# Mask searches that alternate between ScalarE and VectorE, batched transposes and value products, and moved buffers in a two-layer trunk on one core

## The chip, the core and the metric

The kernel runs on one core of a Trainium2 chip. The metric is the device time of one execution in microseconds (us). Engines are named as in the profile: PE is TensorE's matmuls, PEld its weight loads, DVE is VectorE, ACT is ScalarE, POOL is GpSimd, SP is the engine that issues the DMAs.

## What is computed

The input is 2048 tokens of 1024 floats. Layer 0 runs a state-space scan and a convolution module side by side. Layer 1, where the change lies, is sparse attention: a small indexer scores every key for every query, each query keeps its best 256 admissible keys, and attention with 16 query heads over 4 key heads runs on the kept keys alone. Both layers add to their input, and a final norm follows. In short, for layer 1:

```python
isc = relu(einsum("bqhd,bsd->bqhs", qib, ki))        # 8 index heads
score = einsum("bqh,bqhs->bqs", wib, isc)            # -inf beyond the query's chunk of 64
_, idx = top_k(score, 256)
logits = einsum("bqhgd,bqkhd->bqhgk", qb, k[idx]) * 64 ** -0.5
p = softmax(where(valid, logits, -inf))
ob = einsum("bqhgk,bqkhd->bqhgd", p, v[idx])
h = h + (ob * silu(z)) @ w_out
```

## The kernel before

**Stages.** Layer 0 fills about the first third of the span. Layer 1 then works on two halves of 1024 tokens and on 16 query tiles (tile i holds 128 queries and sees (i+1)*128 keys). It projects index queries and keys for half 0 and half 1 (`project_half` with `first`), and, in the same stretch, scores tiles 2 to 15 (`index_scores`) and searches the masks of tiles 2 to 11 (`select_mask`); the other projections (k, v, q, z; `rest`) are emitted after that and fill PE in between. Then comes attention (`Attend`), with the masks of tiles 12 to 15 (`late`) searched beside it, and the output projection (`layer1_out`).

**Who orders the work.** The Tile framework's scheduler puts the instructions of each engine in an order, by readiness and by their place in the program; on the chip each engine then runs its list in that order. `k.after` adds an order between two instructions without a semaphore. Generators mix streams: `index` steps up to three running masks and every second turn the scoring; in attention `weights` steps `late` once for every `PACE` = 800 columns reduced (two columns are counted for each one reduced), 140 steps (`EARLY`) lie ahead of the first unit.

**Mask search** (`select_mask`, L940 to L1055). The score's 32 bits become two 16-bit keys, `khi` and `klo`. The 256th largest key is found bit by bit: count the keys at or above a threshold, and lower the threshold if there are fewer than needed; 16 bits and one more count for each key, so 34 counts a mask. Tiles not in `ON_ACT` count on DVE (L977) and do two small steps per bit on POOL (L69). Tiles 3, 5, 7, 9, 11 and 13 count on ACT with Sign (L994) and do both small steps on ACT too (L1002, L1004). A tail of DVE operations makes the mask (scan at L1048) and stores it.

**Attention** (`Attend`). A unit is one query tile, one pair of key heads (kp) and one pair of query heads (hp): 64 units, each for two key heads e and two query heads h. `weights` multiplies scores into PSUM (L1117), reduces and adds the mask on DVE (L1121), and takes exp on ACT (L1132). `values`, one unit later, goes over groups of two key blocks: four transposes into a PSUM bank (L1148), a copy to SBUF by ACT (L1153; for the largest tiles every second one by DVE, L1151), four products with v (L1155) that use half the array's columns each, in pairs. All products of a unit sum into one bank of the pool `pv`, which has one buffer; `ps_ot`, the transposed output (L1163), takes the same buffer. The transposes' pool `pt` has three banks. SBUF pools are opened and closed like a stack on the left and the right side, so a buffer that lies where an earlier one was waits for that one's last reader. The key and value buffers of half 0 (`kva0`, `kva1`) lie left, where the index stage's buffers were, and are loaded behind the `EARLY` steps; those of half 1 (`kvb0`, `kvb1`) lie first on the right.

Of the kernel before, what the change touches and what calls it, by code (L numbers as in the profile page):

```python
# [23 lines left out]
P = 128  # L24
L = 2048
# [752 lines left out]
def project_half(k, h, hT, new, order, A, h1_d, S, st, rope, ident, identr, vec, pools):  # L778
# [165 lines left out]
def select_mask(k, i, sc, ip, width, chains, mask_d, pace=None, scalar=False):  # L944

# [14 lines left out]
    cnt, rej, th, k2, cl, least, back = (sv[:, a:a + 1] for a in range(7))  # L960
# [32 lines left out]
    def signs(src, nu):  # L993
        nc.scalar.activation(eq, src, AF.Sign, bias=nu, accum_out=cnt)  # L994

    def search_scalar(src, nu):

        nc.vector.memset(nu, 0.5 - 32768.0)
        for b in range(15, -1, -1):
            signs(src, nu)  # L1000
            yield
            nc.scalar.activation(rej, cnt, AF.Sign, bias=least)  # L1002
            yield
            nc.scalar.activation(nu, rej, AF.Identity, bias=nu, scale=-(2.0 ** (b - 1)))  # L1004
            yield
        nc.scalar.activation(rej, nu, AF.Identity, bias=back)
        yield
        signs(src, rej)
        yield

    if scalar:
        nc.vector.memset(back, -0.5)
        nc.vector.memset(least, nk - 2.0 * KSEL + 0.5)
        yield from search_scalar(hi, th)
        k.vts(th, th, -1.0, ALU.mult)
        k.vts(k2, cnt, -0.5, ALU.mult, KSEL - 0.5 * nk, ALU.add)
        k.vts(least, cnt, 2.0 * nk - 2.0 * KSEL + 0.5, ALU.add)
# [5 lines left out]
    if scalar:  # L1023
# [461 lines left out]
```

## Time and profile before

| | us |
|---|---|
| median of 3 runs | 3014.05 (3012.71 to 3017.12) |
| the profiled execution | 3015.91 |
| its span in the profile | 3014.1 |

| engine | busy us in the span | share |
|---|---|---|
| PE | 2753.4 | 91% |
| PEld | 2220.8 | 74% |
| DVE | 2072.8 | 69% |
| ACT | 1733.2 | 58% |
| POOL | 1105.6 | 37% |

The profiled execution is 1.9 us above the median, and 1.8 us of it lie outside the span. Busy time is the union of an engine's instructions; matmul ends are modelled, so the distance between starts is what tells what a matmul costs. An engine's share over the whole span says little here, since stages have different limits; the rows below are by stretch.

### The profile page before, as it was taken

The page shows a single profiled execution, that of the slowest core. Times are in us where ns is not written, and L with a number is a line of the kernel's source. Part 1 is how long each engine was busy: PE and PEld are TensorE (multiplying, and loading weights), DVE is VectorE, ACT ScalarE, POOL GpSimd, SP SyncE. Part 2 cuts the span into 40 slices and gives each one's busy share as a digit, 9 for nine tenths or more (in the row PEclk, how much of TensorE's full clock was granted, in tenths as well). Part 3 has the DMA queues.
Part 4 walks back from the last instruction along what each step waited for, and adds up shares of the span by engine and source line. Part 5 has one row for each costly group of instructions (what it writes and reads, how often), then busy time and mean ns, then how long its engine had stood idle before and what let it go on. Part 6 is the DMA issues. An engine that isn't in the chain of part 4 may idle for free. (4 is left out here: it accounts for less than half of the span.)

```text
span 3014.1 us, 47682 instructions
## 1 busy us (share of the span) xinstructions
PE 2753.4 (91%) x17488; PEld 2220.8 (74%) x17488; DVE 2072.8 (69%) x3735; ACT 1733.2 (58%) x3558; POOL 1105.6 (37%) x1517
## 2 busy tenths in 40 slices
PE   7789998799999999899889968999989999999998
PEld 5667786678999899899779946666655555666787
DVE  8899986995354556644897479734489997456444
ACT  4122332344243688888768957899965666655311
POOL 3946133732232697745774113321232121001000
PEclk9899999899999999999999979999999999999999
DMA  3254563346566323235322261111110101001332
GB/s 134 76 126 142 157 171 63 122 160 208 172 203 226 97 82 120 64 94 175 99 71 82 88 229 38 58 33 37 38 52 26 47 21 53 22 4 50 123 126 98
DMA packets 233385, 300.40 MB, mean 100 GB/s; under 512 B 14144, under 2 KB 171072, under 8 KB 233024
## 3 DMA queue, kind: packets, MB, share of 16 engines
q1 hardware_dynamic: 233152, 297.37, 31.4%
q8 instruction: 137, 2.24, 0.3%
q14 instruction: 96, 0.79, 0.1%
HBM read 194.16 MB, written 105.25 MB: 99 GB/s over the span
## 5 line engine op out<-in xcount | busy, mean ns | idle before, releaser
L114 POOL TENSOR_TENSOR wl<-wst,wh 128x512 fp32r<-128x512 f32 (+1 forms) x220 | 341.5, 1556 | 444.6 <-ACT wh L113 407.9
L121 PE MATMUL ps_tm<-wh,hb 128*128 128x256 f32 (+1 forms) x1536 | 439.3, 290 | 11.7 <-ACT ot L875 6.9
L122 PE MATMUL ps_tm<-wh,hb 128*128 128x256 f32 (+1 forms) x1536 | 444.4, 290 | 0.8 <-DVE hb L72 0.8
L123 PE MATMUL ps_tm<-wl,hb 128*128 128x256 f32 (+1 forms) x1536 | 439.9, 289 | 0.0
L1132 ACT ACTIVATE lm<-lm,mx 128x512 f32<-128x512 f32 (+15 forms) x256 | 309.1, 1209 | 135.0 <-DVE mx L1121 134.4
L1153 ACT COPY pT<-ps_pt 128x512 f32<-128x512 f32 (+1 forms) x512 | 273.6, 563 | 153.0 <-PE ps_pt L1148 127.0
L72 DVE SCALAR_TENSOR_TENSOR cvo<-hc,vec,cvo 128x1024 f32<-128x1024 f32 x240 | 356.0, 1514 | 0.8
L1121 DVE CUSTOM_DVE_ANT_0 lm<-ps_s,amb 128x1024 f32<-128x1024 f32 (+7 forms) x256 | 249.6, 985 | 152.2 <-PE ps_pt L1148 89.4
L1155 PE MATMUL ps_pv<-pT,v 128*64 128x256 f32 x2176 | 339.1, 399 | 14.6 <-DVE avt L62 8.6
L1148 PEld LDWEIGHTS ps_pt<-ident,lm 128*128 128x128 f32 x2176 | 240.1, 141 | 143.1 <-issue 125.0
L1148 PE MATMUL ps_pt<-ident,lm 128*128 128x128 f32 x2176 | 340.8, 282 | 1.8 <-ACT lm L1132 0.7
L1117 PE MATMUL ps_s<-kh,qs 128*128 128x512 f32 (+2 forms) x640 | 268.6, 421 | 48.7 <-DVE mx L1121 42.1
L121 PEld LDWEIGHTS ps_tm<-wh,hb 128*128 128x128 f32 x1536 | 296.2, 194 | 19.6 <-ACT ot L875 9.0
L69 POOL TENSOR_SCALAR sv<-sv 128x1 f32<-128x1 f32 x512 | 185.6, 363 | 321.6 <-DVE eq L977 282.9
L122 PEld LDWEIGHTS ps_tm<-wh,hb 128*128 128x128 f32 x1536 | 298.0, 194 | 6.0 <-DVE hb L72 1.5
L123 PEld LDWEIGHTS ps_tm<-wl,hb 128*128 128x128 f32 x1536 | 296.7, 194 | 4.3
L113 ACT CAST wh<-wst 128x512 fp32r<-128x512 f32 (+1 forms) x220 | 133.2, 609 | 283.2 <-DMA wst<-in_w_in 131.3
L121 PE MATMUL ps_p<-hh,wh 128*128 128x512 f32 x640 | 256.8, 404 | 18.9 <-ACT uT L520 16.5
L123 PE MATMUL ps_p<-hl,wh 128*128 128x512 f32 x640 | 256.9, 404 | 0.0
L122 PE MATMUL ps_p<-hh,wl 128*128 128x512 f32 x640 | 255.9, 400 | 0.0
L977 DVE TENSOR_SCALAR_CACHE_REDUCE eq<-klo,sv 128x384 bf16<-128x384 uint16 (+7 forms) x136 | 207.0, 1525 | 63.5 <-POOL sv L69 62.8
L977 DVE TENSOR_SCALAR_CACHE_REDUCE eq<-khi,sv 128x384 bf16<-128x384 uint16 (+7 forms) x136 | 206.8, 1525 | 48.7 <-POOL sv L69 47.4
(333 smaller groups left out, 6335.2 us busy)
## 6 DMA issues: line engine op xcount, KB each, us to landing
wst<-in_w_in SPq DMA_DIRECT2D x168, 256.0 KB, 2.9
zs_d<-zt SPq DMA_DIRECT2D x16, 512.0 KB, 3.3
zt<-zs_d SPq DMA_DIRECT2D x16, 512.0 KB, 4.4
ry<-rec_d SPq DMA_DIRECT2D x16, 512.0 KB, 4.2
xr<-in_x SPq DMA_DIRECT2D x16, 512.0 KB, 4.4
wst<-in_w_out SPq DMA_DIRECT2D x32, 256.0 KB, 3.4
h_d<-xr SPq DMA_DIRECT2D x16, 512.0 KB, 3.7
xt<-h_d SPq DMA_DIRECT2D x16, 512.0 KB, 5.7
```

The source lines that it names most:

```text
L72: self.nc.vector.scalar_tensor_tensor(out=out, in0=a, scalar=s, in1=b, op0=op0, op1=op1)
L114: nc.gpsimd.tensor_tensor(out=lo, in0=st, in1=hi.bitcast(F32), op=ALU.subtract)
L121: t.matmul(ps, a[0], b[0], start=start, stop=False)
L122: t.matmul(ps, a[1], b[0], start=False, stop=False)
L123: t.matmul(ps, a[0], b[1], start=False, stop=stop)
L977: op = nc.vector.tensor_scalar(out=eq, in0=src, scalar1=u, scalar2=0.0, op0=op, op1=ALU.add, accum_out=cnt)
L1117: nc.tensor.matmul(pss[e][:, cols], qs[e][:, 2 * hp + h], src[:, e, cols], start=part == 0, stop=part == 1)
L1121: self.pace[0] = nc.vector.tensor_tensor_reduce(out=prob[e][h][:, c:c + w], in0=pss[e][:, 0:w], in1=mb[:, c:c + w], scale=-0.125, scalar=( ...
L1132: nc.scalar.activation(lm, lm, AF.Exp, bias=mxs[e, h][:, nh - 1:nh], scale=-1.0, accum_out=t["den"][:, hd:hd + 1])
L1148: nc.tensor.transpose(ps[:, s, h], prob[e][h][:, (b + s) * P:(b + s + 1) * P], ident)
L1153: nc.scalar.copy(pT[:, 0:n], ps[:, 0:n].rearrange("p s h q -> p s (h q)"))
L1155: nc.tensor.matmul(po[64 * s:64 * s + 64, e], self.kvt[(b + s) // 8, kp][2][:, (b + s) % 8, e * 64:e * 64 + 64], pT[:, s], start=b == 0, s ...
```

## The change

Four edits, all in layer 1.

1. **Search.** There is no `ON_ACT` any more. In every mask the odd bits count on ACT with Sign, and their two small steps are on DVE; the even bits and the last count are on DVE, with their small steps on POOL as before. ACT's small steps are gone.
2. **Batches.** `values` takes the groups two at a time (`TURN` = 2). The transposes of a batch come first, then the products of the batch before it; `k.after` holds the first product behind the batch's last transpose, and the next batch's first transpose, also that of the next unit, behind the last product.
3. **Output transposes.** `ps_ot` takes a bank of `pt` in place of the one bank of `pv`.
4. **Buffers and order.** The norm's input tiles become pairs in a pool of two that stays open; the keys of half 0 for kp = 0 take over these two pairs, and are loaded ahead of the `EARLY` steps. v for kp = 0 lies on the right side, loads after the first unit's queries, then the keys and v of kp = 1. The first two tiles run kp = 0 both before kp = 1. On the right side the small pools of attention come first and the half-1 keys last.

```diff
@@ project_half
-            tiles = []
-            for i in range(2):
-                xt = xp.tile([P, D], F32, tag="xt", name="xt1")
+            pair = xp.tile([P, 2, D], F32, tag="xt", name="xt1")
+            tiles = [pair[:, i] for i in range(2)]
+            for i, xt in enumerate(tiles):
                 r0 = h * HALF + (grp * 2 + i) * P
                 nc.sync.dma_start(xt, h1_d[r0:r0 + P])
-                tiles.append(xt)
@@ select_mask
-    def search(src, u, need):
-        nc.vector.memset(u, 32768.0)
+    def search(src, u, need, most):
+        nc.vector.memset(u, 32767.5)
         for b in range(15, -1, -1):
-            count(src, u, ALU.is_ge)
-            yield
-            k.vts(rej, cnt, need, ALU.is_lt, -float(1 << b), ALU.mult, eng=nc.gpsimd)
-            yield
-            k.vts(u, rej, float(1 << (b - 1)) if b else 0.0, ALU.add, u, ALU.add, eng=nc.gpsimd)
+            step = (-float(1 << b), float(1 << (b - 1)) if b else 0.5)
+            if b % 2:
+                nc.scalar.activation(eq, src, AF.Sign, scale=-1.0, bias=u, accum_out=cnt)
+                yield
+                k.vts(rej, cnt, most, ALU.is_gt, step[0], ALU.mult)
+                yield
+                k.stt(u, rej, step[1], u, ALU.add, ALU.add)
+            else:
+                count(src, u, ALU.is_ge)
+                yield
+                k.vts(rej, cnt, need, ALU.is_lt, step[0], ALU.mult, eng=nc.gpsimd)
+                yield
+                k.vts(u, rej, step[1], ALU.add, u, ALU.add, eng=nc.gpsimd)
             yield
...
-    if scalar:
...
-        yield from search_scalar(hi, th)
...
-    else:
-        yield from search(hi, th, KSEL)
-        k.vts(k2, cnt, -1.0, ALU.mult, KSEL, ALU.add)
+    yield from search(hi, th, KSEL, nk - 2.0 * KSEL)
+    k.vts(k2, cnt, -1.0, ALU.mult, KSEL, ALU.add)
+    k.vts(most, cnt, 2.0, ALU.mult, nk - 2.0 * KSEL, ALU.add)
@@ Attend.values
+        def turned(group):
+            e, b = group
...
+                    op = nc.tensor.transpose(ps[:, s, h], prob[e][h][:, (b + s) * P:(b + s + 1) * P], ident)
+                    if self.held is not None:
+                        k.after(op, self.held)
+                        self.held = None
...
+        def weighted(groups, last):
+            for e, b, n, pT, _ in groups:
...
+                    if last is not None:
+                        k.after(op, last)
+                        last = None
+            self.held = op
+        groups = [(e, b) for e in range(2) for b in range(0, nb, 2)]
+        before = None
+        for g in range(0, len(groups), TURN):
+            now = [turned(group) for group in groups[g:g + TURN]]
+            if before:
+                weighted(before, now[-1][4])
+            before = now
+        weighted(before, None)
...
-        ps = self.pv_.tile([P, 2, 2, 128], F32, tag="pv", name="ps_ot")
+        ps = self.pt.tile([P, 2, 2, 128], F32, tag="pt", name="ps_ot")
@@ layer1
-ON_ACT = (3, 5, 7, 9, 11, 13)
+TURN = 2
...
+        xp = pool(ctx, "xp1", 2, side="right")
...
-            xp = pool(c2, "xp1", 4, side="right")
...
-            for kp in range(2):
-                open_kv(0, kp, pool(ctx, f"kva{kp}", 1))
+            kva = pool(ctx, "kva1", 1)
+            open_kv(0, 1, kva, kva)
...
             half(0, False, rest)
+            open_kv(0, 0, xp)
+            load_k(0, 0)
             for _ in range(EARLY):
                 next(beside)
-            load_kv(0)
         with ExitStack() as c3:
-            open_kv(1, 0, pool(c3, "kvb0", 1, side="right"))
-            open_kv(1, 1, pool(c3, "kvb1", 1, side="right"))
-            pp0 = pool(c3, "pp0", 4, side="right")
...
+            qsp, tm = pool(c3, "qsp", 1, side="right"), pool(c3, "tm", 1, side="right")
...
+            v00 = pool(c3, "kva0", 1, side="right").tile([P, 8, 128], F32, name="v00")
...
-            halves = [(i, kp) for i in ORDER for kp in range(2)]
+            a, b = ORDER[0:2]
+            halves = [(a, 0), (b, 0), (a, 1), (b, 1)] + [(i, kp) for i in ORDER[2:] for kp in range(2)]
...
             load(0)
+            load_v(0, 0)
             ready(0)
+            load_k(0, 1)
+            load_v(0, 1)
```

## Rows read from the trace of the kernel before

**Rows 1.** The page of the profile, its line of busy time, share of the span and instructions of each engine, and its line on the chain of waits that ended last, shares by engine.
```profile
PE 2753.4 (91%) x17488; PEld 2220.8 (74%) x17488; DVE 2072.8 (69%) x3735; ACT 1733.2 (58%) x3558; POOL 1105.6 (37%) x1517
...
PE 20%; DVE 6%; issue 3%; POOL 1%; DMA 0%; ACT 0%; DVEq 0%; ACTq 0%; POOLq 0%
```

**Rows 2.** Busy time by stretch (from:to in us, length, then busy us and instructions of PE, PEld, DVE, ACT, POOL, granted clock of TensorE as a share, DMA share, GB/s). From the top: index stage and first projections, two stretches of the remaining projections, the passage into attention, attention while masks are still searched beside it, attention after that, output projection.
```profile
1000.00:1410.00 410.00, 382.36 (x2889) 365.03 (x2889) 232.11 (x504) 346.77 (x907) 272.19 (x441) 0.98 0.34 108
1410.00:1600.00 190.00, 161.49 (x1121) 148.98 (x1120) 175.73 (x247) 133.70 (x298) 142.00 (x221) 0.95 0.25 77
1600.00:1749.00 149.00, 148.25 (x1129) 142.83 (x1128) 82.73 (x130) 139.32 (x304) 35.67 (x42) 1.00 0.28 87
1749.00:1803.00 54.00, 25.78 (x79) 15.36 (x77) 42.36 (x70) 22.02 (x42) 13.00 (x20) 0.65 0.87 302
1803.00:2550.00 747.00, 690.28 (x4402) 456.52 (x4401) 563.21 (x1052) 562.66 (x1085) 188.57 (x393) 0.99 0.12 40
2550.00:2817.00 267.00, 266.31 (x1751) 175.88 (x1750) 144.06 (x258) 151.35 (x213) 31.39 (x35) 1.00 0.09 28
2817.00:3014.00 197.00, 188.15 (x856) 150.51 (x856) 94.09 (x273) 39.51 (x96) 3.14 (x2) 0.99 0.36 125
```

**Rows 3.** The same view for PE alone and single lines over 1803 to 2550 us: matmuls of L1117 (scores, ps_s), L1148 (transposes of the weights, ps_pt), L1155 (value products, ps_pv), L1163 (output transposes, ps_ot) and L772 (query transposes, ps_q), in this order. The count in brackets is used; PE ends are modelled.
```profile
1803.00:2550.00 747.00, 259.95 (x955) 0.99 0.12 40
...
1803.00:2550.00 747.00, 238.25 (x1511) 0.99 0.12 40
...
1803.00:2550.00 747.00, 239.03 (x1512) 0.99 0.12 40
...
1803.00:2550.00 747.00, 30.88 (x208) 0.99 0.12 40
...
1803.00:2550.00 747.00, 28.32 (x216) 0.99 0.12 40
```

**Rows 4.** PE in order of time in a stretch after the last search (start us, us, engine, line, tile, count). The distance from one start to the next is what a run costs; the second column overlaps with what follows.
```profile
2575.86 1.04 PE L1148 MATMUL ps_pt<-ident,lm 128*128 128x128 f32 x8
2576.65 0.48 PE L1117 MATMUL ps_s<-kh,qs 128*128 128x512 f32 x1
...
2577.53 1.95 PE L1155 MATMUL ps_pv<-pT,v 128*64 128x256 f32 x16
2579.40 0.50 PE L1117 MATMUL ps_s<-kh,qs 128*128 128x512 f32 x1
...
2581.47 0.65 PE L1155 MATMUL ps_pv<-pT,v 128*64 128x256 f32 x4
2582.05 0.66 PE L1148 MATMUL ps_pt<-ident,lm 128*128 128x128 f32 x4
2582.63 0.65 PE L1155 MATMUL ps_pv<-pT,v 128*64 128x256 f32 x4
```

**Rows 5.** Waits of the weight loads (PEld: who waited for what, us in total, times, longest), the first four over 1803 to 2550, the last over 2550 to 2817. "issue" is idle time for which the profile shows no releaser.
```profile
PEld ps_pt L1148 <- issue: 85.0, 220, 0.8
PEld ps_s L1117 <- DVE mx L1121: 57.3, 75, 2.6
PEld ps_pv L1155 <- issue: 31.2, 141, 1.6
PEld ps_q L772 <- issue: 9.2, 24, 0.4
...
PEld ps_pt L1148 <- issue: 40.0, 104, 0.4
```

**Rows 6.** Busy time by stretch, columns as in rows 2: one search (17 counts) of mask 13 on ACT, then the searches of masks 14 and 15 on DVE.
```profile
1941.00:2059.00 118.00, 112.27 (x758) 77.61 (x754) 47.15 (x114) 112.01 (x222) 23.54 (x39) 1.00 0.11 36
...
2222.00:2344.00 122.00, 110.75 (x663) 66.21 (x661) 116.41 (x175) 73.89 (x122) 34.23 (x88) 0.99 0.07 24
2382.00:2510.00 128.00, 116.96 (x720) 73.50 (x718) 117.08 (x182) 75.67 (x151) 34.54 (x92) 0.97 0.08 25
```

**Rows 7.** Groups of instructions by line, shapes kept apart (count | busy us, mean ns of one | idle before): the Sign count of mask 13, its accumulator read and its small step on ACT (1941 to 2187 us), the Sign count of mask 11 (1600 to 1749), the DVE count of mask 12 (1790 to 1914), of mask 15 and a small DVE operation on a 128x1 tile (2222 to 2510).
```profile
L994 ACT ACTIVATE eq<-khi,sv 128x1792 bf16<-128x1792 uint16 x17 | 30.6, 1801 | 0.0
...
L1002 ACT ACTIVATE sv<-sv 128x1 f32<-128x1 f32 x32 | 10.1, 317 | 0.0
...
L994 ACT ACTIVATION_READ_ACCUMULATOR eq<-khi,sv 128x1 f32 x17 | 3.4, 201 | 0.0
...
L994 ACT ACTIVATE eq<-khi,sv 128x1536 bf16<-128x1536 uint16 x17 | 26.8, 1579 | 0.2
...
L977 DVE TENSOR_SCALAR_CACHE_REDUCE eq<-khi,sv 128x1664 bf16<-128x1664 uint16 x17 | 33.0, 1939 | 1.9 <-POOL sv L69 1.8
...
L977 DVE TENSOR_SCALAR_CACHE_REDUCE eq<-khi,sv 128x2048 bf16<-128x2048 uint16 x17 | 39.8, 2341 | 2.3 <-POOL sv L69 2.3
...
L67 DVE TENSOR_SCALAR ti<-ti 128x1 int32<-128x1 int32 x3 | 0.5, 151 | 0.0
```

**Rows 8.** The passage from the projections to attention: waits over 1749 to 1803 us (first two rows), and PE in order of time, its first score matmul (start us, us, engine, line, tile, count, idle before and its releaser).
```profile
PE ps_i L906 <- ACT relu L913: 15.0, 6, 6.9
...
DVE scl L69 <- DMA sc_d<-scl: 7.0, 1, 7.0
...
1790.60 0.80 PE L1117 MATMUL ps_s<-kh,qs 128*128 128x512 f32 x1 [4.85 <-ACT qs L774]
```

More of the change, by code (lines that the diff above doesn't have):

```diff
@@ L941, in all_mask, with select_mask @@
     nc.sync.dma_start(mask_d[i, :, 0:nk], eq)
[L944 removed]
+def select_mask(k, i, sc, ip, width, chains, mask_d, pace=None):
     nc = k.nc
@@ L959, in select_mask @@
     sv = ip.tile([P, 8], F32, tag="sv", name="sv", bufs=4)
-    cnt, rej, th, k2, cl, least, back = (sv[:, a:a + 1] for a in range(7))
+    cnt, rej, th, k2, cl, most = (sv[:, a:a + 1] for a in range(6))
     ti = ip.tile([P, 4], I32, tag="ti", name="ti", bufs=4)
@@ L991, in search @@
         yield
[L993 to L1009, printed above, removed]
-    if scalar:
-        nc.vector.memset(back, -0.5)
-        nc.vector.memset(least, nk - 2.0 * KSEL + 0.5)
-        yield from search_scalar(hi, th)
-        k.vts(th, th, -1.0, ALU.mult)
-        k.vts(k2, cnt, -0.5, ALU.mult, KSEL - 0.5 * nk, ALU.add)
-        k.vts(least, cnt, 2.0 * nk - 2.0 * KSEL + 0.5, ALU.add)
-    else:
-        yield from search(hi, th, KSEL)
-        k.vts(k2, cnt, -1.0, ALU.mult, KSEL, ALU.add)
+    yield from search(hi, th, KSEL, nk - 2.0 * KSEL)
+    k.vts(k2, cnt, -1.0, ALU.mult, KSEL, ALU.add)
+    k.vts(most, cnt, 2.0, ALU.mult, nk - 2.0 * KSEL, ALU.add)
     k.stt(y, hi, th, y, ALU.is_equal, ALU.mult)
     yield
-    if scalar:
-        yield from search_scalar(y, cl)
-        k.vts(cl, cl, -1.0, ALU.mult)
-        k.vts(cnt, cnt, 0.5, ALU.mult, 0.5 * nk, ALU.add)
-    else:
-        yield from search(y, cl, k2)
+    yield from search(y, cl, k2, most)
     a, b, c = (ti[:, n:n + 1] for n in range(3))
@@ L1065, in __init__ @@
         self.beside, self.pace, self.cols = beside, pace, 0
-        self.masks = {}
+        self.masks, self.held = {}, None
     def load(self, i, kp):
@@ L1141, in values @@
         po = self.pv_.tile([P, 2, 256], F32, tag="pv", name="ps_pv")
[L1142 to L1157 removed]
+        def turned(group):
+            e, b = group
+            n = min(2, nb - b)
+            ps = self.pt.tile([P, 2, 2, 128], F32, tag="pt", name="ps_pt")
+            for s in range(n):
+                for h in range(2):
+                    op = nc.tensor.transpose(ps[:, s, h], prob[e][h][:, (b + s) * P:(b + s + 1) * P], ident)
+                    if self.held is not None:
+                        k.after(op, self.held)
+                        self.held = None
+            pT = self.ptp.tile([P, 2, 256], F32, tag="pT", name="pT")
+            if b % 4 == 2 and nb > 14:
+                nc.vector.tensor_copy(pT[:, 0:n], ps[:, 0:n].rearrange("p s h q -> p s (h q)"))
+            else:
+                nc.scalar.copy(pT[:, 0:n], ps[:, 0:n].rearrange("p s h q -> p s (h q)"))
+            return e, b, n, pT, op
@@ L1283, in late @@
                     nc.sync.dma_start(sc[:, 0:(j + 1) * P], S["sc"][j, :, 0:(j + 1) * P])
-                    yield from select_mask(k, j, sc, tk, L, 1, S["mask"], pace, scalar=j in ON_ACT)
+                    yield from select_mask(k, j, sc, tk, L, 1, S["mask"], pace)
                     done.add(j)
@@ L1310, in load @@
                 if n == SECOND:
-                    load_kv(1)
+                    for kp in range(2):
+                        load_k(1, kp)
+                        load_v(1, kp)
                 for i, kp in halves[n:n + 1]:
```

54 lines of the change are left out of this document (24 added, 30 removed).

## The prediction, made before the changed kernel was run

> **What bounds the kernel now.** I read the busy line and the chain of waits first [rows 1]: PE is busy 91% of the span and is the chain's largest engine share, but a busy PE is modelled, so I went on to stretches [rows 2]. In the one after the searches (2550 to 2817) PE is busy 266 of 267 us and nothing else is near full. Between 1803 and 2550, with masks searched beside attention, PE, DVE and ACT hold 690, 563 and 563 of 747 us: no engine is full on the average. The split by search tells more [rows 6]: while mask 13 counts on ACT, ACT is busy 112 of 118 us and DVE 47; while masks 14 and 15 count on DVE, DVE is busy 116 of 122 and 117 of 128, and ACT 74 and 76. Each search fills one engine in turn. Earlier, from 1600 to 1749, ACT is busy 139 of 149 us, and in the 54 us from 1749 to 1803 PE is busy 26 and its clock is down to a granted 0.65 [rows 2].
>
> The starts on PE tell what it could do [rows 4]. Eight transposes cost 0.79 us (0.10 each), sixteen value products 1.87 (0.117 each); I take 0.105 for a transpose, as its next neighbour starts late. Four of each by turns cost 2582.63 - 2581.47 = 1.16 us, where the batched prices give 4 x 0.117 + 4 x 0.105 = 0.89. So one run of products between other work costs about 0.27 us more. Such runs show as unexplained idle time in the weight loads that follow: 220 times ahead of transposes and 24 ahead of query transposes up to 2550, 104 times ahead of transposes after it [rows 5].
>
> **PE's work from 1803 to 2550.** Counts [rows 3] by prices: 1512 x 0.117 = 177, 1511 x 0.105 = 159, the small transposes 424 x 0.105 = 45, and 955 score matmuls. Eight of these took 2.07 us with an entry to products in it [rows 4], so at most 0.26; many are narrower than 512 columns, and I take 0.21, 201 us. That is 582 us, and 244 runs x 0.27 = 66. The other 747 - 648 = 99 us are waits; the largest named one is for the reduction on DVE (57 us) [rows 5].
>
> **Batches.** A unit with G groups now has G/2 batches, and the last two batches' products follow each other, so from the code runs are G/2 - 1, at least 1: 232 in 64 units, 152 in tiles up to 12 and 80 in tiles 13 to 15. Up to 2550: (244 - 152) x 0.27 = **-25 us**. After it: (104 - 80) x 0.27 = **-6 us**, all of it on PE's path [rows 2]. Scores may cut a batch, so the ends are 0 and, if some batches join as the runs of sixteen do now, -40 and -12. The strict order takes a freedom away: the second group of a batch needs a bank of `pt` freed while products of the batch before must not yet run. Its cost is not shown; below nothing is excluded, since an order cannot make a copy faster. The nearest row for the other end is the 0.27 us of a change-over itself, over 288 batches 78 us. I take 0, because scores are emitted a unit ahead and fill such gaps; they are the cover, and where they wait for DVE the cost appears.
>
> **Search beside attention.** Sign took 1.58 us on 1536 keys and 1.80 on 1792, so 1.69, 1.80, 1.91, 2.02 for masks 12 to 15; with 0.20 for the accumulator each, 16 odd bits cost ACT 16 x 8.22 = 132 us. Today mask 13 takes 34 x 2.00 + 64 x 0.31 = 88 [rows 7]: ACT +44. DVE counts took 1.94 us on 1664 and 2.34 on 2048, so 2.07 and 2.21 between; today 34 x 6.49 = 221, then 18 x 8.56 = 154 plus 128 small steps x 0.15 = 19 [rows 7]: DVE -48. POOL's small steps halve; DVE stood idle 2.3 us for them in a whole search [rows 7], so they are worth nothing. With 607 and 515 us, ACT and DVE fit into 747 side by side.
>
> The pace changes too. All 64 units count 32 x 17408 = 557,000 columns in about 1014 us, so 800 columns, one step, pass in 1.46 us; a bit has three steps, 4.4 us. Mask 13's 17 counts took 118 us, 6.9 a bit [rows 6], though its own four operations sum to 2.6: they stand in ACT's list behind exps and copies. So it falls behind, and masks 14 and 15 then run as fast as DVE can. Afterwards two bits need 2.1 + 0.3 + 2.3 us and some handing over, within the 8.7 that the pace gives, so there is no catching up. I let the 99 us of waits fall to 60: **-39 us**. Ends: 0 if ACT's load only takes DVE's place, -80 if nearly all go. What is late next is ACT: 607 of the 683 us that remain, 89%; PE has 582 + 41 = 623, 91%.
>
> **Index stage.** From 1600 to 1749 the Sign search of mask 11 and its small steps are 34 x 1.78 + 64 x 0.31 = 80 us of ACT; then 16 x 1.78 = 28 [rows 7]. PE is full there, so nothing is won in it directly, but the scoring of tile 15, which waits for ACT and DVE and runs on after the projections [rows 8], can move ahead of their end. From 1000 to 1600 PE is idle 28 and 29 us [rows 2]; ACT loses small steps and half of some searches, DVE gains small steps where it is already busy 176 of 190. I take **-5**, from -25 to +20.
>
> **Passage.** Of the 54 us, the last matmuls of the index wait 15 us for ACT, and one 7 us wait is for a store of scores, behind the key loads that use the DMA engines 87% of the time; the first score matmul starts at 1790.6 [rows 2, 8]. Now the two 1 MB key loads of kp = 0 need only the norm's buffers, free since the first stage, and go out while the projections run; SP's list then has two fewer big loads at the passage and two v loads behind the first queries. The 12 us or so of index work that move forward still cost PE time. What stays is the chain from the query load over casts, transposes, scores, reduction and exp, and the search's early steps, which now share DVE with ACT. I take 34 us instead of 54: **-20**, ends 0 (the right side's pools now wait for the last projection) and -40.
>
> **The rest.** With `ps_ot` out of `pv` a unit's first product no longer waits for the output's readers, while a bank of `pt` is held for a DVE operation; I put both at 0, within the bounds of the batches. The pairs of norm tiles free two tiles at once: at worst some of the 28 us of PE's idle time in that stage grow, at best nothing; 0. The output projection (197 us) does not change.
>
> **Sum**, from the profiled execution of 3015.9: -25 - 39 - 6 - 5 - 20 = -95, so 2921; the median of the runs is 1.9 lower, so **2919 us**. If every lower end came at once it would be 3014 - 40 - 80 - 12 - 25 - 40 = 2817, and with every upper one 3014 + 78 + 20 = 3112, most of it the batches' unshown wait, against which their cover speaks. Half of the way down is 2868, a third of the way up 2983.
>
> **Rivals.** *ACT becomes the bound* (chance 0.17). Exps and copies stand behind Signs from 1790 on, as in 1941 to 2059, where ACT was at 95% and PE still lost time [rows 6]; the 39 us are not won, nor the 5: 2919 + 44 = **2963**. Against it: Signs are spread over four masks and the small steps are gone.
>
> *The batches are cut* (0.10). The scheduler puts scores between products, or already has the long runs that count: the 31 us go, and with them some cover, another 10: **2960**. For it: runs of sixteen exist today [rows 4].
>
> *DVE waits in its list for Sign* (0.10), the one that ends slower. Today a search on ACT keeps to ACT. Then the small step of each odd bit stands in DVE's list ahead of reductions and cannot start before ACT has come to the Sign. Mask 13's Signs lost 6.9 - 2.6 = 4.3 us a bit to other work of ACT [rows 6, 7]. If DVE stood still for that, 64 odd bits x 4.3 = 275 us come to its 515: 790, or 107 more than the 683. In 1410 to 1600, with three masks, 48 odd bits at half of it are 103 us against 14 us of free DVE [rows 2]: +89. 2919 + 196 = **3115**. With w us of standing still, the loss is 64w - 168 where that is positive, and 48w - 14; it eats the 95 us from about w = 2.3. Against it: the order is planned with ACT's lateness in it, and between two steps lie 800 columns of other work. The Trainium skill, "TensorE: Matmul & The Clock Gate" (Architectural detail), says that ACT's and DVE's queues are strictly first in, first out, while PE can pull weight loads ahead: by that rule this wait would hold every reduction behind it, and the whole 107 us would be paid. The trace agrees in kind: the first score matmul came at 1790.6, with index matmuls ahead of it [rows 8].
>
> *The edits cancel* (0.03): within 0.2%, about what a measurement of this kernel can tell from no change.
>
> **Chances.** The forecast has 0.60. Faster by over 0.2%: 0.60 + 0.17 + 0.10 = 0.87; same 0.03; slower 0.10. The range goes from 2850, a little under half of the way down since the waits could go almost wholly, to 2985, over the two milder rivals; outside are the slow case, the cancelled one and some 0.07 at the lower end.
>
> **What would show it.** Right: pv runs of eight and sixteen and about 230 idle gaps of that kind; from the start of attention to the last search ACT near 90% and DVE near 75%, with no stretch of one at 95% followed by one of the other; ACT under 100 of 149 us before the passage; the kp = 0 key loads issued before the projections end; PE idle under 35 us in the passage. Wrong: long DVE idle time at the small steps released by ACT's Sign, value products or transposes waiting for `pT` copies by more than 0.3 us a batch, or scores of tile 15 still running after the projections.

## The result, and the profile after

The changed kernel took **3051.99 us** (median of 4 runs, 3044.33 to 3057.48) beside 3015.59 us of the kernel before on the same chip: ratio **1.0115** (95% interval 1.0098 to 1.0132). It is slower by some 36 us where 2919 us was forecast. The profiled execution has a span of 3052.2 us, 38.1 more than before.

The page's busy line and chain answer to [rows 1]: every engine's busy time is within 43 us of what it was, and PE's is 12 us lower, so the 38 us are time in which PE stands idle.

```profile
PE 2741.1 (90%) x17488; PEld 2232.1 (73%) x17488; DVE 2115.2 (69%) x4121; ACT 1695.6 (56%) x3202; POOL 1122.5 (37%) x1453
...
PE 36%; DVE 20%; issue 7%; ACT 6%; POOL 6%; DMA 4%; SPq 0%; DVEq 0%; ACTq 0%; POOLq 0%
```

Of the windows of [rows 2], in the changed kernel (attention cut at 2200):

```profile
1000.00:1410.00 410.00, 371.67 (x2755) 349.49 (x2754) 325.28 (x782) 323.84 (x743) 293.87 (x465) 0.99 0.28 86
...
1600.00:1749.00 149.00, 132.72 (x924) 122.18 (x923) 113.57 (x180) 86.11 (x164) 64.78 (x75) 0.98 0.32 101
1749.00:1803.00 54.00, 48.30 (x346) 44.35 (x344) 42.59 (x65) 27.51 (x49) 11.46 (x16) 1.00 0.33 105
1803.00:2200.00 397.00, 328.51 (x2062) 228.84 (x2064) 269.76 (x567) 299.59 (x557) 102.43 (x189) 0.94 0.17 58
```

Three things are to be seen. From 1000 to 1410 VectorE is busy 325 us where it was 232. From 1600 to 1749 PE is busy 133 us where it was full (148): projections have slid into the 54 us behind, which were nearly empty before. And from 1803 to 2200 PE is busy 329 of 397 us, ACT 300, DVE 270: no engine is near full, and PE waits (19 of the 397 us lie ahead of attention's first matmul).

Two marks on PE split each span into three parts: up to the start of the first score matmul, attention (from there to the start of the last value product), and the rest to the end. Before: 1790.6 + 1025.3 + 198.2. After: 1821.9 + 1021.4 + 208.9, which is **+31.3, -3.9 and +10.7**. All experiments are read by these marks. The first one varied from -3 to +7 us between kernels with the same code ahead of it, so a few us in one trace mean nothing.

The waits of PE in attention (1790 to 2845; who waited for what, us, times, longest) show what PE waits for now. The names: `pT` is the copy of transposed weights, `ov` the copy of a unit's summed products, `avt` one of VectorE's two multiplications that read the output transposes, `rd` VectorE's reciprocal ahead of them, `qs` ScalarE's cast of the query transposes, `mx` the reduction's result.

```profile
PE ps_s L1094 <- DVE mx L1098: 27.0, 43, 1.8
...
PE ps_pt L1127 <- ACT qs L774: 9.7, 15, 1.1
PE ps_pt L1127 <- ACT pT L1135: 8.1, 13, 1.9
PE ps_pt L1127 <- DVE avt L62: 8.1, 7, 1.8
PE ps_pv L1142 <- ACT pT L1135: 8.0, 10, 1.3
PE ps_ot L1164 <- ACT ov L1160: 7.4, 8, 2.1
PE ps_pt L1127 <- DVE rd L1167: 4.4, 4, 3.1
```

Of the kernel before the same view (1790 to 2815) has these rows on scores, products, output transposes and transposes:

```profile
PE ps_s L1117 <- DVE mx L1121: 42.1, 50, 4.8
PE ps_pv L1155 <- DVE avt L62: 8.6, 13, 1.4
...
PE ps_ot L1163 <- ACT ov L1159: 1.2, 2, 1.1
...
PE ps_pt L1148 <- ACT qs L774: 0.5, 1, 0.5
PE ps_pt L1148 <- ACT pT L1153: 0.3, 1, 0.3
```

The scores' wait for the reduction fell. Transposes of the weights hardly ever waited; now they wait 30.3 us in these rows, 22.2 of them for readers of the other tenants of their banks: `avt` and `rd` (VectorE, output transposes), `qs` (ScalarE, query transposes). The order of time at one change of units shows how:

```profile
1897.07 1.81 ACT L985 ACTIVATE eq<-klo,sv 128x1792 bf16<-128x1792 uint16 x1
...
1898.59 1.08 PE L1142 MATMUL ps_pv<-pT,v 128*64 128x256 f32 x8
...
1900.29 2.08 DVE L975 TENSOR_SCALAR_CACHE_REDUCE eq<-klo,sv 128x1792 bf16<-128x1792 uint16 x1
...
1901.12 0.58 ACT L1160 COPY ov<-ps_pv 128x512 f32<-128x512 f32 x1
...
1901.75 0.66 PE L1164 MATMUL ps_ot<-ident,ov 128*128 128x128 f32 x4 [2.07 <-ACT ov L1160]
1902.16 0.88 PE L772 MATMUL ps_q<-identr,tmq 128*128 128x128 f32 x8
...
1903.21 1.79 ACT L985 ACTIVATE eq<-klo,sv 128x1792 bf16<-128x1792 uint16 x1 [0.38 <-POOL sv L69]
1903.29 0.41 DVE L62 TENSOR_TENSOR avt<-ps_ot,zr 128x256 f32<-128x256 f32 x1
...
1903.85 1.09 PE L1127 MATMUL ps_pt<-ident,lm 128*128 128x128 f32 x4 [0.80 <-DVE avt L62]
...
1905.62 1.12 PE L1127 MATMUL ps_pt<-ident,lm 128*128 128x128 f32 x4 [0.69 <-ACT qs L774]
```

The eight products end a unit. Their copy `ov` stands in ScalarE's list behind a Sign and two exps, and PE stands 2.07 us at the output transposes. These and the query transposes then hold all three banks; the next transposes wait for VectorE's two multiplications, which stand behind a count of 2.08 us, and the ones after for ScalarE's cast, behind another Sign. PE lost 3.6 us here, at one of 64 such places; it is a bad one, since the waits of output transposes and transposes above come to 0.6 us a place. The Trainium skill, "TensorE: Matmul & The Clock Gate" (Part 3, The mechanism), says that matmuls are strictly first in, first out; the stretch agrees, since no matmul passed the four output transposes in the 2.07 us that they waited.

### The profile page after: what moved, and what is told of

It reads as the page before. It is cut to its first block, busy times and chain, and to the rows that moved or that the text cites. A ratio compares the mean times of both kernels' runs of the same rounds, so it can differ in the third digit from the quotient of the medians.

```text
span 3052.2 us, 47596 instructions
## 1 busy us (share of the span) xinstructions
PE 2741.1 (90%) x17488; PEld 2232.1 (73%) x17488; DVE 2115.2 (69%) x4121; ACT 1695.6 (56%) x3202; POOL 1122.5 (37%) x1453
## 4 chain that ended last, share of the span: by engine, by line
PE 36%; DVE 20%; issue 7%; ACT 6%; POOL 6%; DMA 4%; SPq 0%; DVEq 0%; ACTq 0%; POOLq 0%
PE ps_pt L1127 7%; PE ps_pv L1142 7%; DVE eq L975 7%; PE ps_s L1094 7%; DVE lm L1098 2%; PE ps_o L122 2%; POOL sv L69 2%; PE ps_o L121 2%; PE ps_o L123 2%; ACT eq L985 2%; PE ps_tm L121 2%; PE ps_tm L122 2%; PE ps_tm L123 2%; POOL wl L114 2%; DVE scl L72 2%
## 5 line engine op out<-in xcount | busy, mean ns | idle before, releaser
L1127 PE MATMUL ps_pt<-ident,lm 128*128 128x128 f32 x2176 | 317.5, 282 | 33.5 <-ACT qs L774 9.7
L1109 ACT ACTIVATE lm<-lm,mx 128x1024 f32<-128x1024 f32 (+15 forms) x256 | 307.9, 1205 | 60.2 <-DVE mx L1098 55.2
L1142 PE MATMUL ps_pv<-pT,v 128*64 128x256 f32 x2176 | 318.8, 395 | 8.3 <-ACT pT L1135 8.0
L1094 PE MATMUL ps_s<-kh,qs 128*128 128x512 f32 (+2 forms) x640 | 269.5, 422 | 30.1 <-DVE mx L1098 27.0
L1094 PE MATMUL ps_s<-kl,qs 128*128 128x512 f32 (+2 forms) x640 | 235.5, 373 | 0.0
L1142 PEld LDWEIGHTS ps_pv<-pT,v 128*64 128x64 f32 x2176 | 136.8, 136 | 112.7 <-issue 48.4
```

The costliest lines, as they stand in the source:

```text
L1094: nc.tensor.matmul(pss[e][:, cols], qs[e][:, 2 * hp + h], src[:, e, cols], start=part == 0, stop=part == 1)
L1109: nc.scalar.activation(lm, lm, AF.Exp, bias=mxs[e, h][:, nh - 1:nh], scale=-1.0, accum_out=t["den"][:, hd:hd + 1])
L1127: op = nc.tensor.transpose(ps[:, s, h], prob[e][h][:, (b + s) * P:(b + s + 1) * P], ident)
L1142: op = nc.tensor.matmul(po[64 * s:64 * s + 64, e], self.kvt[(b + s) // 8, kp][2][:, (b + s) % 8, e * 64:e * 64 + 64], pT[:, s], start=b == ...
```

## The experiments

| kernel | ratio to before (95%) | first score | attention | rest |
|---|---|---|---|---|
| the change | 1.0115 (1.0098 to 1.0132) | +31.3 | -3.9 | +10.7 |
| e1 search alone | 0.9953 (0.9932 to 0.9973) | +19.1 | -30.1 | +0.1 |
| e2 value part alone | 1.0082 (1.0053 to 1.0112) | +0.3 | +20.8 | +2.6 |
| e3 buffers alone | 1.0003 (0.9990 to 1.0016) | -13.1 | +6.1 | +8.2 |
| e4 all but search | 1.0083 (1.0060 to 1.0107) | -7.5 | +23.0 | +9.3 |
| e5 batches without edges | 1.0089 (1.0069 to 1.0109) | -3.1 | +30.8 | +1.0 |
| e6 batches, bank as before | 1.0037 (1.0025 to 1.0050) | +7.4 | +10.5 | 0.0 |
| e7 bank alone | 1.0166 (1.0146 to 1.0185) | -1.3 | +50.5 | +0.4 |
| e8 all but the value part | 1.0021 (1.0007 to 1.0034) | +28.8 | -29.8 | +8.9 |
| e9 change, bank as before | 0.9979 (0.9966 to 0.9992) | +30.6 | -45.7 | +10.0 |
| e10 batches, no edges, bank as before | 0.9951 (0.9937 to 0.9966) | -3.0 | -9.9 | 0.0 |
| e11 turns in masks 12 to 15 | 0.9919 (0.9903 to 0.9936) | -3.4 | -20.1 | +0.3 |
| e12 change, EARLY 100 | one run, 3049.18 us | +19.8 | +3.6 | +9.9 |
| e13 e10 and e11 | 0.9957 (0.9941 to 0.9974) | +2.9 | -19.5 | 0.0 |
| e14 e9 without edges | 0.9925 (0.9909 to 0.9941) | +31.7 | -57.1 | +8.4 |
| e15 change without edges | 1.0162 (1.0144 to 1.0180) | +36.4 | +7.8 | +10.5 |
| e16 bank of its own | 1.0204 (1.0180 to 1.0227) | -1.9 | +62.0 | +0.1 |
| e17 turns in masks 2 to 11 | 1.0103 (1.0082 to 1.0124) | +38.7 | -8.2 | 0.0 |
| e18 e1 and e10 | **0.9892** (0.9872 to 0.9912) | +24.7 | -49.2 | 0.0 |

The three right columns are us against the kernel before, each from one trace. The traced run lies within 4 us of its kernel's median, but for e13, where it is the fastest of six and 9.7 us below it.

**Which edit costs (e1 to e4).** Each takes whole functions from one of the two kernels: e1 has `select_mask` of the change, e2 its `Attend`, e3 only its pools and loads, e4 everything but `select_mask`.

> The kernel before with the new mask search alone. Theory S (the search that alternates between ACT and DVE makes each search stand in three engines' lists, and every list stands still for the others): the last projection comes some 40 us later as in the changed kernel, attention has more waits, 3035 to 3065 us in all. Rival T (the strict order of batches costs the waits in attention, and the search is harmless): 3000 to 3020 us. Rival M (the moved buffers delay the projections): also 3000 to 3020 us.

> The kernel before with the batches and the output transposes in the transposes' banks alone. Theory S: the change-overs saved show, about 290 runs of value products in place of some 400, 2980 to 3000 us. Rival T: the order makes PE wait for copies and banks, 3015 to 3040 us though the runs are as few.

> The kernel before with the moved buffers, the key loads and the order of the first units alone. Theory S: the passage from the last projection to the first scores shrinks by about 20 us, the end loses about 10 us where the output projection starts later, 3000 to 3010 us. Rival M: the projections end some 30 us later because of the buffers, 3030 to 3045 us.

> The changed kernel with the old search (odd tiles on ACT, the others on DVE and POOL). Theory S: everything that the other parts give is left, 2960 to 2995 us, faster than before and some 60 to 80 us faster than the changed kernel. Rivals T and M: 3025 to 3050 us, as the changed kernel.

The search gained on balance, so theory S falls as a whole, though one of its signs is there: in e1 the last projection starts 52 us later than before. The value part alone cost 24 us in its trace, as rival T has it. The buffers cost nothing on balance, as sums of a gain and two losses; e3 met neither expectation. e4 stays as slow as rivals T and M have it.

**What in the value part (e7, e5, e6, e10, e16).** The edits, on the kernel before (e7) and on e2 (e5 drops the two `k.after`, e6 puts the bank back, e10 does both); e16 is e7 with a bank of its own:

```diff
-        ps = self.pv_.tile([P, 2, 2, 128], F32, tag="pv", name="ps_ot")
+        ps = self.pt.tile([P, 2, 2, 128], F32, tag="pt", name="ps_ot")     # e7
+        ps = self.pot.tile([P, 2, 2, 128], F32, tag="po", name="ps_ot")    # e16
-                     pool(c3, "pt2", 3, space=PSUM), pool(c3, "pv", 1, space=PSUM))
+                     pool(c3, "pt2", 2, space=PSUM), pool(c3, "pv", 1, space=PSUM),
+                     pool(c3, "pot", 1, space=PSUM))                       # e16
```

In the diff, the constructor's line of e16 that takes the new pool is left out.

> The kernel before with the batched value part, but without the two order edges: the program emits two groups of transposes and then two groups of products, and the ordering of the scheduler alone decides what TensorE does next; the output transposes stay in the transposes' banks. The batches with both edges gave ratio 1.0082 (+22 us in the profile, all of it in attention). Theory O (the edges cost: TensorE stands at a product or a transpose that may not pass, while ScalarE runs a Sign): at most half of the loss is left, ratio 0.998 to 1.004, and the waits of the transposes for ScalarE's pT and qs copies (11.3 and 8.4 us in attention) fall below 8 us together, while the runs of products go back toward 400. Theory C (two batches of transposes hold two of the three banks, and the later copies free the exp buffers late, with or without the edges): ratio 1.006 to 1.010, attention still 1040 us or more.

> The kernel before with the batches and both order edges, but the output transposes in the value products' bank as they were. Theory P (a third kind of tenant in the transposes' three banks makes the transposes of the next unit wait for VectorE's avt and ScalarE's ov): the 9.1 us of transposes waiting for avt and the 11.3 us of output transposes waiting for ov shrink, ratio 1.000 to 1.004. Theory O: the edges remain and the bank of the value products comes free later (the next unit's products wait for the avt product of VectorE, 31.2 us of such waits in the kernel before), so nothing is won: ratio 1.006 to 1.012.

> The kernel before with one line changed: the output transposes take a bank of the transposes' three instead of the value products' one. No batches, no edges. Theory P: slower by itself, ratio 1.003 to 1.006 (9 to 18 us), with new waits of transposes for VectorE's avt. Theory O: no loss, ratio 0.997 to 1.001, the 31.2 us wait of the value products for their bank shrinks.

> The kernel before with the value part emitted in batches of two groups, but without the order edges and with the output transposes in the value products' bank: the batch alone. With the edges it gave 1.0037 (attention 1036 us against 1025). With the output transposes in the transposes' banks the edges made no difference that could be measured (1.0089 without, 1.0082 with). If the batch itself costs (both banks of a batch must be copied by ScalarE before its products, and the exp buffers are read out later): ratio 1.002 to 1.006, as with the edges. If the edges are what costs there: 0.996 to 1.001.

> The kernel before with the output transposes in a bank of their own, and two banks instead of three left for the transposes and query transposes. Ring theory (the ring of the shared banks is handed out in program order, so the next unit's transposes stand behind the output transposes): with a ring of its own the output transposes hold nobody up, and the ratio is below that of the shared ring with three banks (1.0166): 0.998 to 1.008. Shortage theory (transposes with effectively one bank fewer cost the 50 us): with two banks always it is as slow or slower, 1.014 to 1.03.

One line, the bank of the output transposes, costs 50.5 us of attention by itself, more than the change as a whole loses and more than either theory of e7 allowed. (The 31.2 us that the expectations of e6 and e7 put down to products waiting for `avt` are the row of idle "issue" time in [rows 5]; for `avt` it is 8.6 us.) The edges are not the cause: without them e2 is no faster (e5, as the batch theory has it). With the bank put back, half the loss is gone though the edges stay (e6), and without edges the batches win 9.9 us of attention (e10, a little past its better expectation); there the edges cost 20.4.

Two theories were left for the bank: that the ring of shared banks is handed out in program order and holds the next unit's transposes behind the output transposes, or that transposes are short of a bank. e16 expected 0.998 to 1.008 by the first and 1.014 to 1.03 by the second; 1.0204 bears out the second, though e16 takes a bank from the transposes for good, and e7 only while the output transposes hold it. The waits over 1790 to 2815, of e16 first, then e7 (whose attention runs on to 2876 and 2865), show the products waiting for ScalarE's copies and more change-overs; the kernel before has 3.9 us in 7 waits and 125.0 us in 324 in the two rows of e16:

```profile
PE ps_pv L1155 <- ACT pT L1153: 23.1, 30, 1.4
...
PEld ps_pt L1148 <- issue: 173.3, 448, 0.8
```

```profile
PE ps_ot L1163 <- ACT ov L1159: 10.5, 16, 2.8
PE ps_pv L1155 <- ACT pT L1153: 10.0, 16, 1.5
PE ps_pt L1148 <- DVE avt L62: 6.4, 7, 2.6
...
PEld ps_pt L1148 <- issue: 142.5, 358, 2.8
```

With less room to run ahead, transposes and products alternate more: by the starts in the traces there are 401 runs of products (products with no other matmul between) in attention before, 476 in e7, 557 in e16. Transposes of the next unit stand right ahead of the output transposes in 28 of 64 units before, in none in e7, and in 28 again in e16; anywhere behind the unit's last product, they go ahead in nearly every unit before and in e16, and in none in e7. So e7 has the fixed order of the first theory, and e16 is slow without it. No run gives the output transposes a bank of their own beside three for the transposes, so how much of e7's loss is that order is open. How e7's 50 us divide was not measured. An estimate: 75 more runs at the prediction's 0.27 us are 20 us, and PE's waits at output transposes, products and transposes rose by some 21 us (10.5 against 1.2 for `ov`, 10.0 against 3.9 for `pT`, 6.4, 5.4 and 2.8 for `avt`, `qs` and `rd` where there was 0.5, less the 8.6 that products waited for `avt`). For the 41.8 us between the changed kernel and e9 the same sum does not come out, since the changed kernel has fewer runs (303 against 331).

**The same in the changed kernel (e9, e14, e15).** e9 is the changed kernel with the one line of the bank put back, e14 that without the edges, e15 the changed kernel without the edges.

> The changed kernel with one line put back: the output transposes use the value products' bank again. Search by turns, batches with both order edges and moved buffers stay. Theory P (the ring of three transposes' banks is handed out in program order, so with the output transposes in it the next unit's transposes can no longer go ahead of them on TensorE while ScalarE copies ov): attention, 1021 us in the changed kernel, falls by 8 to 20 us; ratio to the kernel before 1.005 to 1.009 (the changed kernel: 1.0115), and transposes stand again between the last product and the output transposes of some 20 units or more. Theory O (what costs beside the search is the strict order, and the search's Signs make it worse): attention within 5 us of 1021, ratio 1.010 to 1.013.

> The changed kernel with the output transposes back in the value products' bank and without the two order edges. With the edges it gave 0.9979. On the kernel before the edges cost 26 us in this arrangement (1.0037 with, 0.9951 without). If they cost the same beside the search by turns: ratio 0.988 to 0.992. If the search's gain already contains it, since VectorE no longer holds the scores up: 0.996 to 1.000.

> The changed kernel without the two order edges, all else as it is (output transposes in the transposes' banks). Theory P (the ring of banks orders TensorE already, so the edges add nothing): ratio 1.009 to 1.014, as the changed kernel's 1.0115. Theory O (beside the Signs the edges are what costs): 1.000 to 1.005.

The one line turns 1.0115 into 0.9979, and attention from 1021.4 to 979.6 us, more than twice what either theory expected (transposes stand between the last product and the output transposes of nearly every unit again, right ahead of the latter in 12). The waits of e9 (1790 to 2815): no transpose waits for `avt` any more and they wait 0.3 us for `qs`, while the products pay a little for sharing their bank.

```profile
PE ps_pv L1142 <- DVE avt L62: 7.2, 14, 2.4
PE ps_pv L1142 <- ACT pT L1135: 5.8, 8, 1.1
PE ps_ot L1164 <- ACT ov L1160: 3.2, 3, 1.2
PE ps_pt L1127 <- ACT pT L1135: 2.8, 3, 1.5
```

The edges cut both ways. In the changed kernel they help by 12 us of attention (e15 missed both expectations on the slow side), and with the old bank they cost 11 (e14, its first expectation but for a little).

**Ahead of attention (e8, e12, e11, e17).** e8 is the changed kernel with `Attend` of before. e11 and e17 keep both versions of the search in the kernel before and use the turns in the late masks or in the index stage alone (masks 2 to 11; the expectation says 3 to 11, but mask 2 counts by turns too).

```diff
-EARLY = 140
+EARLY = 100    # e12, on the changed kernel
```

> The changed kernel with the value part as it was before (no batches, no edges, output transposes in their old bank): search by turns and moved buffers stay. Theory V (all of the loss comes from the value part and from its meeting with the search): ratio 0.993 to 0.997, about the search alone (0.9953), since the buffers alone gave 1.0003. Theory M (the meeting of search and buffers costs, the later end of the projections taking back what the passage gave): ratio 0.998 to 1.004.

> The changed kernel with 100 instead of 140 search steps emitted ahead of attention, so that the load of mask 13's scores is not in SyncE's list ahead of the first mask and query loads. In the changed kernel that load waited 7.0 us for the end of mask 12's search, the first mask load was issued at 1805.1, and the first query transposes came 18 us after the last projection. Theory Q (SyncE's list): first mask load at 1799 to 1801, right behind the last projection at 1799, and first score matmul at 1815 to 1818 instead of 1821.9. Theory H (they wait for the space of the projections' inputs alone): no change, 1820 to 1823.

> The kernel before, with the search by turns for masks 12 to 15 alone (beside attention); masks 3 to 11 are searched as before, on ScalarE or VectorE, in the index stage. Theory I (in the index stage the search by turns costs: VectorE is fuller there, index matmuls wait for it and for ScalarE, and TensorE idles some 20 us more between 1300 and 1700; the gain is beside attention): the first score matmul comes at 1788 to 1793 as before, attention takes 1000 to 1015 us, the ratio is 0.988 to 0.994 (the search in all masks: 0.9953). Theory W (attention wins in the search-alone kernel only because mask 12 is searched 100 us earlier, in the projections; the turns themselves win nothing): first score matmul as before and attention 1020 to 1030 us, ratio 0.998 to 1.002.

> The kernel before with the search by turns for masks 3 to 11 alone (index stage); masks 12 to 15 are searched as before. If the index stage's search by turns costs (e11, its complement, had its first score matmul at 1787 and attention at 1005 us; all masks by turns had 1810 and 995): first score matmul at 1803 to 1812, mask 12's score load about 100 us earlier than in the kernel before, attention 1010 to 1020 us, ratio 1.000 to 1.005. If the late start was due to mask 12's turns falling into the projections (in all-by-turns they ran from 1690 to 1795): first score matmul 1790 to 1798 and ratio 0.994 to 0.999.

e8 met the expectation of theory M: search and buffers lose by meeting. e11 met theory I: beside attention the turns themselves gain. Turns in the index stage cost: e17's first score came 38.7 us late, e11's 3.4 early; e17 is slower than its expected 1.000 to 1.005. With mask 12 by turns as well (e1) the first score is 19.1 us late; why it is later in e17 is open. In the window 1600 to 1749, of e17 and then of e11, PE is full only where the old search runs:

```profile
1600.00:1749.00 149.00, 127.62 (x881) 116.09 (x880) 125.89 (x181) 69.64 (x141) 64.03 (x94) 0.99 0.29 92
```

```profile
1600.00:1749.00 149.00, 146.63 (x1105) 140.15 (x1103) 82.31 (x124) 137.93 (x301) 33.66 (x37) 1.00 0.29 91
```

The index matmuls' waits for ScalarE's relu over 1000 to 1800 rose from the first row (before) to the second (e17). VectorE is fuller, and it also stands at its small steps for ScalarE's Sign: over 1000 to 1825 the third row (e17) and the fourth (the changed kernel), against 2.9 us in e11. No run takes that wait away, so which operation holds the index stage was not settled.

```profile
PE ps_i L906 <- ACT relu L913: 45.8, 39, 6.9
```

```profile
PE ps_i L906 <- ACT relu L913: 61.3, 68, 3.5
```

```profile
DVE sv L69 <- ACT eq L1100: 49.3, 39, 3.2
```

```profile
DVE sv L69 <- ACT eq L985: 78.0, 63, 3.2
```

Why buffers and search together lose the buffers' gain: in e3 the first score comes 13.1 us earlier; attention's first buffers lie where the projections' inputs were, but the last projection (1744.3) lies 30 us ahead of the last index matmul there. With the search by turns the projections end last (1799.3), so the loads come only then. And the load of mask 13's scores stands ahead of them in SyncE's list, waiting for the last read of mask 12's (SyncE's wait, its issues, and the first score matmul, which answers to [rows 8], in the changed kernel):

```profile
SPq L1286 <- DVE eq L72: 7.0, 1, 7.0
```

```profile
1804.67 0.33 SPq L1286 DMA_DIRECT2D scr<-sc_d  x1
1805.06 0.41 SPq L1053 DMA_DIRECT2D amb<-mask_d  x1
```

```profile
1821.93 0.79 PE L1094 MATMUL ps_s<-kh,qs 128*128 128x512 f32 x1 [2.57 <-ACT qs L774]
```

In e12 that load is out of the way (theory Q), the mask load goes out from 1797.18 on and the first score comes 11.5 us earlier, more than expected; attention gives 7.5 of it back. What the mask load waits for in e12 is a projection (SyncE's wait over 1785 to 1815):

```profile
SPq L1053 <- PE ps_tm L123: 4.7, 1, 4.7
```

**Together (e13, e18).**

> The kernel before with the two parts that gained by themselves: search by turns for masks 12 to 15 alone (0.9919) and the value part in batches without order edges, output transposes in the value products' bank (0.9951). No moved buffers. If they add up: ratio 0.985 to 0.989. If the batches lose what they gain once ScalarE runs Signs beside attention (two copies are needed before a batch's products): 0.990 to 0.995.

> The kernel before with the search by turns in all masks and the value part in batches without order edges, output transposes in the value products' bank; no moved buffers. The same with moved buffers gave 0.9925, and beside the search by turns those cost 20 us (1.0021 against 0.9953). If that adds up: 0.984 to 0.988, the best version. If the batches win less beside the search, as with the search in late masks (0.9957 together, 0.9919 without batches): 0.990 to 0.996.

e11 and e10 do not add up: together (0.9957) they are slower than e11, and than either expectation. e18, between its two, with turns in all masks, the batches without edges, the old bank and no moved buffers, is the fastest version measured: 2988.23 us, 1.1% below the kernel before and some 2% below the change, though it still loses 24.7 us ahead of attention.

## Why the prediction was wrong

The forecast's -95 us and the measured +38 of the span lie 133 us apart: 66 in attention (-70 forecast, -3.9 measured), 56 ahead of it (-25, +31.3) and 11 behind it (0, +10.7). So two steps failed, and in small a third, the output projection.

**The first step that failed** stands under "The rest": that a bank of `pt` is held for a VectorE operation was put "at 0, within the bounds of the batches". Shown, it is 50.5 us alone (e7) and 41.8 in the changed kernel (e9). No row stood for the 0: of the two sides, a product that no longer waits for the output's readers could give back 8.6 us on PE, while nothing was asked of what the transposes lose with their bank. e16 points to the bank that they then lack; how far the order of the shared banks adds to it is open.

**The second step that failed** is the index stage, put at -5 with +20 as its worst end. Turns there make the first score 38.7 us late by themselves (e17) and 19.1 with all masks by turns (e1). VectorE was forecast to gain small steps; it is busy 93 us more from 1000 to 1410 alone. With the bank put back (e9) the time is 3014.03 us, still outside the range, with 30.6 us lost ahead of attention.

**Batches: right sign, half the size.** -31 was predicted; alone they gave -9.9 (e10), with 327 runs of products instead of 401, 74 x 0.27 = 20 us of change-overs. About half of that is missing; the waits of PE that grew most are those for the reduction (49.1 us in e10, 42.1 before) and for `avt` (11.3, 8.6). In the changed kernel there are 303 runs; without those that only score matmuls cut, 234, as the 232 of the forecast. The idle gaps fell too, though some moved to the scores: over 1790 to 2815 in the kernel before, then over 1822 to 2844 in the changed kernel:

```profile
PEld ps_pt L1148 <- issue: 125.0, 324, 0.8
...
PEld ps_s L1117 <- issue: 6.4, 17, 0.4
```

```profile
PEld ps_pt L1127 <- issue: 73.5, 171, 3.2
...
PEld ps_s L1094 <- issue: 31.4, 82, 0.4
```

That such a change-over costs at all, the Trainium skill, "TensorEngine Tiling (Array Packing)" (Key Properties), gives as a drain of TensorE when the tiling mode changes; the rows agree so far as time is lost there, about 0.27 us a run [rows 4, 5].

**The strict order.** Taken as 0, with the scores as cover: measured -12 to +20 us of attention, by the bank beside it. Where the order cost most (e6 against e10, 20.4 us), products waited longer for `avt` (19.8 against 11.3 us); the rest of that cost is open.

**Search beside attention: right, smaller.** -39 predicted, -20.1 with the same masks left over (e11), -30.1 with mask 12 moved ahead (e1). ACT and DVE are busy 610 and 534 us in e11 from 1803 to 2550 (607 and 515 predicted). The loads' waits for the reduction fell, as expected; over 1790 to 2815, before and e11:

```profile
PEld ps_s L1117 <- DVE mx L1121: 65.1, 81, 5.5
```

```profile
PEld ps_s L1209 <- DVE mx L1213: 33.5, 59, 1.7
```

**Rival of the slower side.** The wait of VectorE's small steps for Sign is there, 41.2 us in the changed kernel and 20.4 in e1 over 1790 to 2815. The 48 odd bits of masks 13 to 15 fall there (mask 12 is searched before), so that is 0.86 and 0.43 us each, where the rival has it decide from 2.3 on. Beside attention the rival's cause is not the cause of the loss: e1 has the wait and gains 30.1 us. Ahead of attention, where the 78.0 us above stand, it is not ruled out. The trace row that the prediction gives for in-order queues [rows 8] shows PE alone; these rows show VectorE standing at the step. ACT became no bound either, at 299.6 of 397 us.

```profile
DVE sv L69 <- ACT eq L985: 41.2, 31, 3.3
```

**Index stage and passage.** -5 and -20 predicted, +31.3 measured for both. The stretch from the last projection to the first product did shrink, 56 to 38 us, but its start moved from 1748.2 to 1799.3: the forecast's 54 us were not idle time at the end of a chain, index matmuls ran on in them until 1780.4. The right mark was the first score matmul. Seen by it, the buffers alone gave the 13 us.

**The output projection "does not change":** +10.7, of which 8.2 come with the buffers (e3). By the order of the pools its weights are staged on the left, where the keys and v of half 0 lie. Before, the first casts came at 2761.6; in e3 only the buffers of `kp` = 1 lie there, which attention reads until near its end. The casts that stage the weights, before and in e3 (first and last start), and the first operation behind them in e3, which waited 12.0 us for a value product:

```profile
L1358 ACT CAST wo<-wst x8: 1032/1048/1057, 2761.6 to 2822.8; 128x1024 fp32r<-128x1024 f32 x8
```

```profile
L1370 ACT CAST wo<-wst x8: 1044/1048/1050, 2804.1 to 2828.5; 128x1024 fp32r<-128x1024 f32 x8
```

```profile
2805.40 4.69 POOL L62 TENSOR_TENSOR wo<-wst,wo 128x1024 fp32r<-128x1024 f32 x2 [12.01 <-PE ps_pv L1154]
```

So the first output matmul comes 1 us ahead of the last value product in e3, and 19 us ahead of it before.

## What to carry to other kernels

Price every tenant of a small set of PSUM banks by how long its reader's engine lets it wait, and look at what ran ahead in those banks before; a bank taken from the tile that runs ahead can cost more than the whole change gains elsewhere. Judge a stretch between two marks only if neither mark moves, and follow each moved buffer to the next stage that reuses its space.

## What the runs showed that was not expected

The same two order edges gained 10 to 12 us of attention with the output transposes in the transposes' banks and cost 11 to 20 with them outside: what a fixed order is worth depends on the banks beside it. (The 10, e2 against e5, is from one trace each; the ratios of these two do not differ.) And parts that gain alone need not add: turns in the late masks (-20.1) and free batches (-9.9) gave -19.5 together, while turns in all masks (-30.1) and free batches gave -49.2.
